# Softmax sums by matmuls, and HGRN2 keys and queries relative to chunk references, in a hybrid encoder layer

## The chip, the core and the metric

The kernel runs on one core of a Trainium2 chip. The metric is device time in microseconds (us) of one execution; less is better. Engines are named as the profile names them: PE (matrix engine; PEld is its weight load), DVE (vector), ACT (scalar, activation functions), POOL (GpSimd), SP (issues most of the DMAs).

## What is computed

One layer of an encoder for 512 tokens of width 1024. Two branches read the same normalised input: grouped-query attention with 8 heads of 64 and 2 key/value heads, and a gated linear recurrence (HGRN2) with 4 heads of 128, run once forward and once backward. Both are gated, added, projected and added to the input; a mixture of 32 experts in 4 groups follows. The change touches the softmax and the recurrence:

```
p = softmax(q k^T * scale);  o = p v                      # per head
f = lb + (1 - lb) * sigmoid(z);  k = (1 - lb) * sigmoid(-z)
b = cumsum(log f) within chunks of 32;  b_ref = b[16];  b_last = b[31]
a = (q * exp(b - b_ref)) (k * exp(b_ref - b))^T, masked;  o_intra = a v
o_inter = (q * exp(b)) state;  state = exp(b_last) * state + (k * exp(b_last - b))^T v
```

## The kernel before

Input projections come first, as products of float32 numbers split into a high and a low float32r part, three matmuls per product (`mm3`, L257 to L260; weights are split by ACT on L250 and DVE on L251). Then a loop over four HGRN heads h (L631) does for each h: the attention scores of heads 2h and 2h+1 (`att_scores`), the recurrence forward and backward (`hgrn_dir`), some other projections, the attention output of the pair (`att_out`), and the recurrence's output. Then come the branch projections with their gates, the output projection, the router, and the experts, whose 1 MB weight pieces are streamed through a ring of buffers as matmuls free them.

The program is written in this order, but a scheduler orders the instructions of PE, DVE, ACT and POOL ahead of time by its own estimate of durations; on the chip each engine then works strictly in that order. Only SP's queue stays as written.

In `att_scores` (L406) the keys lie on the partitions: four score tiles of 128 keys x 512 queries per head. DVE takes the maximum of the four (L423), POOL takes it over the partitions (`partition_all_reduce`, L424), DVE subtracts (L426) and ACT exponentiates (L427). For the denominator POOL adds the four tiles in pairs (L429, L430), DVE adds the two sums (L431), and one matmul with a matrix of ones adds over the partitions (L434). That matmul writes 64 of the 128 partitions, one half of the bank per head of the pair; ACT forms the reciprocal as exp(-ln) once for the pair (L437, L438). `att_out` multiplies the probabilities with v (L447, eight matmuls, the two heads alternating between the halves) and scales (L449).

In `hgrn_dir` (L505) the features lie on the partitions and the 512 tokens on the free axis: 4 blocks of 128 tokens with 4 chunks of 32 each. DVE clips the projection (L513), ACT forms log f in four passes (L514 to L517), POOL adds z and ln(1+exp(-z)) (L518), DVE sums within chunks by a scan (L520), which overwrites what L518 reads. Three exponent tiles follow (L530 to L534) and four wide exps (L532, L535 to L537): keys and queries relative to the chunk's reference (`z`, `e1`), keys to the chunk's end (`b`) and queries from its start (`e3`). One exp of the 16 chunk ends gives the chunks' decays T (L526), and POOL multiplies them up to the factors between the chunks of a block (L550 to L558). Scaled by them, keys and queries become `k2`, `q2`, `kt`, `qt` (L566 to L572). PE transposes `kt` (L586) and forms the blocks' states (L591). Back in the loop PE forms all decayed products between keys and queries in small matmuls (L661, L665), DVE masks them (L668 to L674), and PE forms the output (L685).

Of the kernel before, what the change touches and what calls it, by code (L numbers as in the profile page):

```python
# [11 lines left out]
ALU = mybir.AluOpType  # L12
# [92 lines left out]
def program_(tc, A, out, dbg=None):  # L105
# [41 lines left out]
    def ps(tag="b"):  # L147
        return tl(PS, [P, 512], tag, bufs=banks[tag])
# [254 lines left out]
    pq, den = [None], [None]  # L403
    probs = {}

    def att_scores(h):  # L406
# [22 lines left out]
        G.tensor_tensor(mx, sc[0], sc[1], op=ALU.add)  # L429
        G.tensor_tensor(mr, sc[2], sc[3], op=ALU.add)  # L430
        V.tensor_tensor(mx, mx, mr, op=ALU.add)  # L431
        if h % 2 == 0:
            den[0] = ps("po")
        PE.matmul(den[0][a], ones[:, 0:64], mx, start=True, stop=True)  # L434
        if h % 2 == 1:
            rc = at()
            SA.activation(rc, den[0], AF.Ln)  # L437
            SA.activation(rc, rc, AF.Exp, scale=-1.0)  # L438
            probs["r", h // 2] = rc
        probs[h] = sc  # L440

    def att_out(m):

        o = ps("po")
        for j in range(NT):
            for i in range(2):
                PE.matmul(o[HALF[i]], vt[:, j, m // 2], probs[2 * m + i][j], start=(j == 0), stop=(j == NT - 1))  # L447
        rc = probs["r", m]
# [44 lines left out]
    zero = tl(RH, [P, P], "zero")  # L493
    G.memset(zero, 0.0)

    FAC = [[tl(RH, [P, 2, 4, NT], "fac%d%d" % (d_, i)) for i in range(2)] for d_ in range(2)]
    for d_ in range(2):
        for i in range(2):
            G.memset(FAC[d_][i], 1.0)

    def c4(ap):

# [2 lines left out]
    def hgrn_dir(h, d_, q):  # L505
# [3 lines left out]
        z = tl(RH, [P, 512], "z", bufs=2)  # L509
        u = tl(RH, [P, 512], "k", bufs=2)  # L510
        b = tl(RH, [P, 512], "bb", bufs=2)
        p_ = proj_fm(3 * h + d_)
        V.tensor_scalar(z, p_, -ZMAX, None, op0=ALU.max)  # L513
        SA.activation(u, z, AF.Exp, scale=-1.0)  # L514
        SA.activation(b, u, AF.Ln, bias=1.0)
        SA.activation(u, b, AF.Exp, scale=-1.0)
        SA.activation(u, u, AF.Ln, bias=lb[:, d_, h:h + 1], scale=omb[:, d_, h:h + 1])  # L517
        G.tensor_tensor(z, z, b, op=ALU.add)  # L518
        bv, uv = (b, u) if fw else (b[:, ::-1], u[:, ::-1])
        V.tensor_tensor_scan(bv, scanm, uv, 0.0, op0=ALU.mult, op1=ALU.add)  # L520
# [7 lines left out]
        e1 = tl(RH, [P, 512], "e1", bufs=2)
        e3 = tl(RH, [P, 512], "e3", bufs=2)
        V.tensor_tensor(z, z, b, op=ALU.add)  # L530
        V.tensor_tensor(uc, bc_, b3(bc_[:, :, ir], 16, 32), op=ALU.subtract)
        SA.activation(e1, u, AF.Exp)  # L532
        V.tensor_tensor(uc, b3(bc_[:, :, it], 16, 32), zc, op=ALU.subtract)
        V.tensor_tensor(zc, b3(bc_[:, :, ir], 16, 32), zc, op=ALU.subtract)  # L534
        SA.activation(z, z, AF.Exp, bias=lo_)  # L535
        SA.activation(e3, b, AF.Exp)
        SA.activation(b, u, AF.Exp, bias=lo_)  # L537
        V.scalar_tensor_tensor(e1, q, SC_H, e1, op0=ALU.mult, op1=ALU.mult)
        V.scalar_tensor_tensor(e3, q, SC_H, e3, op0=ALU.mult, op1=ALU.mult)

        ch = [0, 1, 2, 3] if fw else [3, 2, 1, 0]
        t4 = T.rearrange("p (t c) -> p t c", c=4)
        t_ = [t4[:, :, c] for c in ch]
        fac = FAC[d_][h % 2]
        kf = [fac[:, 0, c] for c in ch]
        qf = [fac[:, 1, c] for c in ch]
        whole = tl(RH, [P, NT], "whole", bufs=2)

        def mul(o, x, y):
            G.tensor_tensor(o, x, y, op=ALU.mult)  # L550

        G.tensor_copy(kf[2], t_[3])
        G.tensor_copy(qf[1], t_[0])
        mul(kf[1], t_[3], t_[2])
        mul(qf[2], t_[0], t_[1])
        mul(kf[0], kf[1], t_[1])
        mul(qf[3], qf[2], t_[2])
        mul(whole, kf[0], t_[0])  # L558
# [8 lines left out]
        V.tensor_tensor(q2[:, :, ch[3] % 2], c4(e3)[:, :, ch[3]], b3(t_[2], NT, 32), op=ALU.mult)
# [3 lines left out]
        V.tensor_tensor(c4(kt), c4(b), b4(fac[:, 0].rearrange("p c t -> p t c")), op=ALU.mult)
        G.tensor_tensor(c4(qt), c4(e3), b4(fac[:, 1].rearrange("p c t -> p t c")), op=ALU.mult)  # L572
# [20 lines left out]
        V.tensor_copy(st[:, 0], pu[:, 0:P])  # L593
        for n_ in (1, 2):
            i = order[n_]
            V.scalar_tensor_tensor(st[:, n_], st[:, n_ - 1], whole[:, i:i + 1], pu[:, n_ * P:(n_ + 1) * P],
                                   op0=ALU.mult, op1=ALU.add)
        return e1, z, qt, st, blocks


    def gate(chunk):
# [625 lines left out]
```

## Time and profile before

| | |
|---|---|
| median of 3 runs | 982.7 us (977.29 to 982.86) |
| profiled execution | 979.89 us |
| its span | 978.0 us |
| mean granted PE clock | 0.967 |
| DMA moved | 246.52 MB |

The profile shows one execution. Its page gives the busy time of each engine, the span in 40 slices with a digit of busy share each, the granted PE clock, and groups of instructions by line. Views of the trace give the same for stretches of time, the waits of one engine for another, and single instructions in order of time. A float32 matmul is shown as two records. In a row of a group "x8 | 11.4, 1420 | 22.6 <-" means eight instructions, 11.4 us busy, 1420 ns each, 22.6 us of idle time of the engine ahead of them and what ended it.

### The profile page before, as it was taken

The page shows a single profiled execution, that of the slowest core. Times are in us where ns is not written, and L with a number is a line of the kernel's source. Part 1 is how long each engine was busy: PE and PEld are TensorE (multiplying, and loading weights), DVE is VectorE, ACT ScalarE, POOL GpSimd, SP SyncE. Part 2 cuts the span into 40 slices and gives each one's busy share as a digit, 9 for nine tenths or more (in the row PEclk, how much of TensorE's full clock was granted, in tenths as well). Part 3 has the DMA queues.
Part 4 walks back from the last instruction along what each step waited for, and adds up shares of the span by engine and source line. Part 5 has one row for each costly group of instructions (what it writes and reads, how often), then busy time and mean ns, then how long its engine had stood idle before and what let it go on. Part 6 is the DMA issues. An engine that isn't in the chain of part 4 may idle for free. (4 is left out here: it accounts for less than half of the span.)

```text
span 978.0 us, 12665 instructions
## 1 busy us (share of the span) xinstructions
PE 884.4 (90%) x5058; PEld 560.2 (57%) x5059; DVE 456.1 (47%) x804; ACT 276.8 (28%) x476; POOL 154.2 (16%) x174
## 2 busy tenths in 40 slices
PE   6899779798796999999779999999989989899896
PEld 5889667586573888889743444444334443343333
DVE  6999769696764445442532332322213222132214
ACT  6557646466563344442201000000000000000000
POOL 4543343342521001110100000000000000000000
PEclk9999979998897999999969999999999999999999
DMA  6212101111010223499459999999999999999994
GB/s 217 97 66 87 65 25 48 59 44 65 24 65 22 86 86 107 151 413 406 142 211 379 388 421 417 419 419 418 419 418 419 419 419 419 417 420 420 420 405 136
DMA packets 49647, 246.52 MB, mean 252 GB/s; under 512 B 7088, under 2 KB 12976, under 8 KB 25648
## 3 DMA queue, kind: packets, MB, share of 16 engines
q1 hardware_dynamic: 44160, 238.32, 60.9%
q0 software_dynamic: 2304, 4.20, 1.2%
q10 hardware_dynamic: 3120, 3.15, 0.9%
q8 instruction: 42, 0.69, 0.3%
q14 instruction: 21, 0.17, 0.0%
HBM read 245.64 MB, written 4.19 MB: 255 GB/s over the span
## 5 line engine op out<-in xcount | busy, mean ns | idle before, releaser
L1034 PE MATMUL b<-e,wr 128*64 128x512 f32 x728 | 204.6, 600 | 8.6 <-DMA e<-in_wu 8.2
L1034 PEld LDWEIGHTS b<-e,wr 128*64 128x64 f32 x728 | 61.3, 137 | 105.3 <-issue 86.0
L1041 ACT ACTIVATE gt<-b,sw 128x512 f32<-128x512 f32 x16 | 11.0, 687 | 328.7 <-PE b L1034 328.7
L1059 PE MATMUL b<-e,gt 128*64 128x512 f32 (+1 forms) x368 | 95.4, 576 | 8.0 <-DMA e<-in_wd 6.1
L260 PE MATMUL b<-x,wl 128*128 128x512 f32 x224 | 90.8, 406 | 3.3 <-DVE wl L251 3.3
L258 PE MATMUL b<-x,wh 128*128 128x512 f32 x224 | 90.5, 404 | 3.1 <-DVE hg L481 2.2
L1034 PE MATMUL b<-x,wr 128*64 128x512 f32 x264 | 90.5, 597 | 2.7 <-DMA x<-in_wu 2.7
L1062 DVE TENSOR_TENSOR t<-b,t 128x512 fp32r<-128x512 f32 (+1 forms) x33 | 22.2, 673 | 147.9 <-ACT t L1061 147.9
L259 PE MATMUL b<-x,wh 128*128 128x512 f32 x224 | 90.0, 402 | 0.0
L250 ACT ACTIVATE wh<-wr 128x1024 fp32r<-128x1024 f32 (+1 forms) x60 | 61.5, 1027 | 78.2 <-PE b L259 44.5
L251 DVE TENSOR_TENSOR wl<-wr,wh 128x1024 fp32r<-128x1024 f32 (+1 forms) x60 | 77.1, 1286 | 10.7 <-ACT wh L250 10.7
L1005 POOL DMA_INDIRECT xs<-xd,ix x16 | 16.2, 1014 | 335.8 <-DVE sw L1007 179.9
L1059 PEld LDWEIGHTS b<-e,gt 128*64 128x64 f32 x368 | 30.8, 137 | 60.0 <-issue 46.1
L1042 DVE SCALAR_TENSOR_TENSOR gt<-b,sw,gt 128x512 f32<-128x512 f32 x16 | 12.0, 751 | 105.7 <-PE b L1034 95.6
L258 PE MATMUL b<-wh,m 128*128 128x256 f32 x176 | 51.2, 294 | 10.4 <-ACT wh L250 6.2
L1059 PE MATMUL b<-x,gt 128*64 128x512 f32 x152 | 50.6, 594 | 3.6 <-DMA x<-in_wd 3.6
L259 PE MATMUL b<-wl,m 128*128 128x256 f32 x176 | 51.6, 294 | 2.1 <-DVE wl L251 1.9
L1061 ACT ACTIVATE t<-b 128x512 fp32r<-128x512 f32 (+1 forms) x33 | 19.3, 584 | 120.3 <-PE b L1059 120.3
L260 PE MATMUL b<-wh,m 128*128 128x256 f32 x176 | 51.0, 292 | 1.3 <-DVE m L185 1.3
L260 PEld LDWEIGHTS b<-x,wl 128*128 128x128 f32 x224 | 43.6, 195 | 14.7 <-DVE wl L251 4.6
L1078 PE MATMUL b<-t,wl 128*128 128x512 f32 (+1 forms) x132 | 51.4, 391 | 0.0
L1079 PE MATMUL b<-t,wl 128*128 128x512 f32 (+1 forms) x132 | 50.5, 384 | 0.4 <-DVE t L1062 0.4
(326 smaller groups left out, 1679.6 us busy)
## 6 DMA issues: line engine op xcount, KB each, us to landing
e<-in_wu SPq DMA_DIRECT2D x46, 1024.0 KB, 19.9
e<-in_wg SPq DMA_DIRECT2D x45, 1024.0 KB, 19.9
e<-in_wd SPq DMA_DIRECT2D x42, 1024.0 KB, 19.9
x<-in_wd SPq DMA_DIRECT2D x19, 1024.0 KB, 19.9
x<-in_wg SPq DMA_DIRECT2D x17, 1024.0 KB, 19.9
x<-in_wu SPq DMA_DIRECT2D x16, 1024.0 KB, 19.9
wr<-in_wfm SPq DMA_DIRECT2D x28, 512.0 KB, 3.5
wr<-in_wtok SPq DMA_DIRECT2D x12, 512.0 KB, 3.4
```

The costliest lines, as they stand in the source:

```text
L250: SA.activation(h_[:, ks], r[:, ks], AF.Copy)
L251: V.tensor_tensor(l_[:, ks], r[:, ks], f(h_)[:, ks], op=ALU.subtract)
L258: PE.matmul(o, ah, bh, start=first, stop=False)
L259: PE.matmul(o, ah, bl, start=False, stop=False)
L260: PE.matmul(o, al, bh, start=False, stop=last)
L1005: G.indirect_dma_start(xs[q % 2][:, b], None, xd[:, :], bass.IndirectOffsetOnAxis(ap=ix[:, b], axis=0), bounds_check=S - 1, oob_is_err=False)
L1034: PE.matmul(o[j * 64:(j + 1) * 64, :], hT[half][:, k, b * P + j * 64:b * P + (j + 1) * 64], ring[(n, e, half)](k), start=(half == 0 and k ...
L1059: PE.matmul(o[j * 64:(j + 1) * 64, 0:w], hidT[:, k * P + j * 64:k * P + (j + 1) * 64], ring[("wd", e, n)](k)[:, c:c + w], start=(k == 0), ...
L1061: SA.activation(y[:, 2 * n, c:c + w], o[:, 0:w], AF.Copy)
L1062: V.tensor_tensor(y[:, 2 * n + 1, c:c + w], o[:, 0:w], f(y)[:, 2 * n, c:c + w], op=ALU.subtract)
L1078: PE.matmul(p_[:, 0:w], l, y[:, 2 * n, c:c + w], start=(i == 0), stop=False)
L1079: PE.matmul(p_[:, 0:w], l, y[:, 2 * n + 1, c:c + w], start=False, stop=(i == len(ys) - 1))
```

## The change

*Softmax.* The additions L429 to L431 and the two single matmuls per pair are taken out. `att_out` now accumulates the denominators: for each of the four key tiles and each head of the pair, a matmul with ones, into the bank that the transposed queries use (`pq`, one buffer). Ln and Exp follow, then the output matmuls.

*Keys and queries.* The scan writes over `z` instead of the logarithms. Only two wide exps remain: of b - b_ref and of its negative. The keys come from POOL's product of exp(-z) and sigmoid(z), times (1 - lb). The decays between chunks are formed as logarithms: POOL copies the chunk ends, DVE scans them over the block and adds the references, POOL subtracts three sets of differences, and ACT takes one exp of 72 numbers per partition. Keys and queries of all chunks (`kt`, `qt`) and those of the products between chunks (`k2`, `q2`, now two and three chunks wide) are scaled by these.

```
     def att_out(m):
-        o = ps("po")
+        o, den = ps("po"), ps("pq")
+        for j in range(NT):
+            for i in range(2):
+                PE.matmul(den[HALF[i]], ones[:, 0:64], probs[2 * m + i][j], start=(j == 0), stop=(j == NT - 1))
+        rc = at()
+        SA.activation(rc, den, AF.Ln)
+        SA.activation(rc, rc, AF.Exp, scale=-1.0)
...
     def hgrn_dir(h, d_, q):
...
-        SA.activation(u, b, AF.Exp, scale=-1.0)
-        SA.activation(u, u, AF.Ln, bias=lb[:, d_, h:h + 1], scale=omb[:, d_, h:h + 1])
-        G.tensor_tensor(z, z, b, op=ALU.add)
-        bv, uv = (b, u) if fw else (b[:, ::-1], u[:, ::-1])
-        V.tensor_tensor_scan(bv, scanm, uv, 0.0, op0=ALU.mult, op1=ALU.add)
+        SA.activation(s_, b, AF.Exp, scale=-1.0)
+        SA.activation(b, s_, AF.Ln, bias=lb[:, d_, h:h + 1], scale=omb[:, d_, h:h + 1])
+        G.tensor_tensor(u, u, s_, op=ALU.mult)
+        zv, bv = (z, b) if fw else (z[:, ::-1], b[:, ::-1])
+        V.tensor_tensor_scan(zv, scanm, bv, 0.0, op0=ALU.mult, op1=ALU.add)
...
+        V.tensor_tensor(b.rearrange("p (c s) -> p c s", s=32), zc, b3(zc[:, :, ir], 16, 32), op=ALU.subtract)
+        SA.activation(e1, b, AF.Exp)
+        SA.activation(s_, b, AF.Exp, scale=-1.0)
...
+        G.tensor_copy(ends[:, :, 1:5], way(c4(z)[:, :, :, it]))
+        V.tensor_tensor_scan(L[:, 0:NT * 5], starts.rearrange("p t c -> p (t c)"), ends.rearrange("p t c -> p (t c)"),
+                             0.0, op0=ALU.mult, op1=ALU.add)
+        R = Y[:, :, 4:8]
+        V.tensor_tensor(R, way(c4(z)[:, :, :, ir]), X[:, :, 0:4], op=ALU.add)
+        G.tensor_tensor(Y[:, :, 0:4], X[:, :, 4:5].to_broadcast([P, NT, 4]), R, op=ALU.subtract)
+        G.tensor_tensor(Y[:, :, 8:11:2], R[:, :, 1:4:2], R[:, :, 0:3:2], op=ALU.subtract)
+        G.tensor_tensor(Y[:, :, 11:13], R[:, :, 2:3].to_broadcast([P, NT, 2]), R[:, :, 0:2], op=ALU.subtract)
+        SA.activation(E, L, AF.Exp)
...
+        V.scalar_tensor_tensor(e1, q, SC_H, e1, op0=ALU.mult, op1=ALU.mult)
+        V.scalar_tensor_tensor(u, u, omb[:, d_, h:h + 1], s_, op0=ALU.mult, op1=ALU.mult)
...
+        V.tensor_tensor(c4(kt), c4(u), b4(way(EY[:, :, 0:4])), op=ALU.mult)
+        G.tensor_tensor(c4(qt), c4(e1), b4(way(EY[:, :, 4:8])), op=ALU.mult)
+        V.tensor_tensor(k2, c4(u)[:, :, 0:2] if fw else c4(u)[:, :, 2:4], b4(way(EY[:, :, 11:13])), op=ALU.mult)
+        V.tensor_tensor(q2, c4(e1)[:, :, 1:4] if fw else c4(e1)[:, :, 0:3], b4(way(EY[:, :, 8:11])), op=ALU.mult)
```

The matmuls of the recurrence keep their number and shapes. In the changed file L518 becomes L524 (POOL's product), L520 L526, L434 L435 and L447 L441; the copy of the ends is L540, the small scan L541, the three subtractions L545 to L547, the masks L663 to L669, the transposes L581, and L685 L680.

The scheduler's order moves with it. On POOL, around the all-reduces of attention heads 2 and 3 (`at`), before; ISA rows are instructions of POOL's own:

```order
L424 ISA
L424 ISA at_1394<-at_1393 128x512
L429 ISA
L429 TENSOR_TENSOR at_1393<-m_1389,m_1390 128x512
L430 TENSOR_TENSOR at_1394<-m_1391,m_1392 128x512
L424 ISA
L424 ISA at_1560<-at_1559 128x512
L429 ISA
L429 TENSOR_TENSOR at_1559<-m_1555,m_1556 128x512
L430 TENSOR_TENSOR at_1560<-m_1557,m_1558 128x512
```

and in the changed kernel:

```order
L424 ISA
L424 ISA at_1389<-at_1388 128x512
L424 ISA at_1542<-at_1541 128x512
L524 ISA
L524 TENSOR_TENSOR k_1967<-k_1967,sg_1969 128x512
L540 COPY end_135_837<-z_1966 128x4x4
L545 TENSOR_TENSOR log_131_833<-log_131_833 128x4x4
```

With the additions gone the two all-reduces follow each other, and what comes behind them is the product and the copy for the next forward direction. The same holds for heads 6 and 7; heads 0, 1, 4 and 5 keep other POOL work between.

On DVE, between the first pair's output and the second forward direction (`as` and `zb` are the masked products, `m` the score tiles), before:

```order
L513 TENSOR_SCALAR z_1466<-b_1475 128x512
L670 COPY_PREDICATED as_1346<-c_maskf_282,zero_831 128x512
L426 TENSOR_TENSOR m_1015<-m_1015,at_1020 128x512
L426 TENSOR_TENSOR m_1016<-m_1016,at_1020 128x512
L426 TENSOR_TENSOR m_1017<-m_1017,at_1020 128x512
L426 TENSOR_TENSOR m_1018<-m_1018,at_1020 128x512
L520 SCALAR_TENSOR_TENSOR bb_1468<-c_scanm_286,k_1467 128x512
L668 COPY_PREDICATED zb_829<-c_maskb_284,hg_1281 128x128
L530 TENSOR_TENSOR z_1466<-z_1466,bb_1468 128x512
L531 TENSOR_TENSOR k_1467<-bb_1468 128x512
L674 TENSOR_TENSOR as_1346<-as_1346,zb_829 32x4x32 x4
```

and in the changed kernel:

```order
L663 COPY_PREDICATED zb_829<-c_maskb_284,hg_1276 128x128
L665 COPY_PREDICATED as_1341<-c_maskf_282,zero_831 128x512
L669 TENSOR_TENSOR as_1341<-as_1341,zb_829 32x4x32 x4
L426 TENSOR_TENSOR m_1013<-m_1013,at_1018 128x512
L426 TENSOR_TENSOR m_1014<-m_1014,at_1018 128x512
L426 TENSOR_TENSOR m_1015<-m_1015,at_1018 128x512
L426 TENSOR_TENSOR m_1016<-m_1016,at_1018 128x512
L519 TENSOR_SCALAR z_1456<-b_1467 128x512
L251 TENSOR_TENSOR wl_1654<-wr_1649,wh_1653 128x1024
L526 SCALAR_TENSOR_TENSOR z_1456<-c_scanm_286,bb_1458 128x512
L529 TENSOR_TENSOR bb_1458<-z_1456 128x512
L541 SCALAR_TENSOR_TENSOR log_132_834<-starts_841,end_136_838 128x20
```

The masks moved ahead of the subtractions and the scan; the small scan that needs POOL's copy stands behind the large one.

On PE, the last pair's sums and outputs (`po` and `pq` are the banks, `m` the probability tiles, `sc` a branch projection, `hg` the recurrence's output), before:

```order
L665 MATMUL hg_2905<-e_455_2705,z_2662 32x32 x16
L434 MATMUL po_2492<-at_2625,ones_82 64x512
L447 MATMUL po_2892<-m_2455,vt_161 64x512
L447 MATMUL po_2892<-m_2621,vt_161 64x512
L447 MATMUL po_2892<-m_2456,vt_161 64x512
L447 MATMUL po_2892<-m_2622,vt_161 64x512
```

and in the changed kernel, behind one matmul of each kind 50 rows earlier:

```order
L260 MATMUL sc_2973<-t_827,wl_2955 128x512
L435 MATMUL pq_2828<-m_2571,ones_82 64x512
L435 MATMUL pq_2828<-m_2419,ones_82 64x512
L441 MATMUL po_2827<-m_2571,vt_161 64x512
L441 MATMUL po_2827<-m_2419,vt_161 64x512
L435 MATMUL pq_2828<-m_2572,ones_82 64x512
L435 MATMUL pq_2828<-m_2420,ones_82 64x512
L441 MATMUL po_2827<-m_2572,vt_161 64x512
```

The sums now read the probabilities (`m`) instead of POOL's and DVE's sum (`at`), stand behind 18 branch matmuls, and are mixed with the outputs.

More of the change, by code (lines that the diff above doesn't have):

```diff
@@ L402, in program_ @@
     aTh, aTl = [tl(U, [P, 4, 512], "t", F32R, bufs=2) for _ in range(2)]
-    pq, den = [None], [None]
+    pq = [None]
     probs = {}
@@ L427, in att_scores @@
             SA.activation(sc[j], sc[j], AF.Exp, scale=0.125)
[L429 to L439, printed above, removed]
         probs[h] = sc
     def att_out(m):
-        o = ps("po")
+        o, den = ps("po"), ps("pq")
[5 more added lines that the diff above has]
+        SA.activation(rc, rc, AF.Exp, scale=-1.0)
         for j in range(NT):
@@ L494, in program_, with logs @@
     G.memset(zero, 0.0)
-    FAC = [[tl(RH, [P, 2, 4, NT], "fac%d%d" % (d_, i)) for i in range(2)] for d_ in range(2)]
+    LOGS = [[tl(RH, [P, NT * 18], "log%d%d" % (d_, i)) for i in range(2)] for d_ in range(2)]
+    ENDS = [[tl(RH, [P, NT, 5], "end%d%d" % (d_, i)) for i in range(2)] for d_ in range(2)]
+    starts = tl(RH, [P, NT, 5], "starts")
+    G.memset(starts, 1.0)
+    G.memset(starts[:, :, 0], 0.0)
     for d_ in range(2):
         for i in range(2):
-            G.memset(FAC[d_][i], 1.0)
+            G.memset(LOGS[d_][i], 0.0)
+            G.memset(ENDS[d_][i], 0.0)
+    def logs(t):
+        return (t[:, 0:NT * 5].rearrange("p (t c) -> p t c", c=5), t[:, NT * 5:].rearrange("p (t c) -> p t c", c=13))
     def c4(ap):
@@ L528, in hgrn_dir @@
[L528 to L558, printed above, removed]
+        V.tensor_tensor(b.rearrange("p (c s) -> p c s", s=32), zc, b3(zc[:, :, ir], 16, 32), op=ALU.subtract)
+        SA.activation(e1, b, AF.Exp)
+        SA.activation(s_, b, AF.Exp, scale=-1.0)
+        L, ends = LOGS[d_][h % 2], ENDS[d_][h % 2]
+        X, Y = logs(L)
@@ new lines, in hgrn_dir, with way @@
+        E = tl(RH, [P, NT * 18], "fac", bufs=2)
+        def way(ap):
+            return ap if fw else ap[:, :, ::-1]
+        G.tensor_copy(ends[:, :, 1:5], way(c4(z)[:, :, :, it]))
[4 more added lines that the diff above has]
+        G.tensor_tensor(Y[:, :, 0:4], X[:, :, 4:5].to_broadcast([P, NT, 4]), R, op=ALU.subtract)
@@ L572, in hgrn_dir @@
-        G.tensor_tensor(c4(qt), c4(e3), b4(fac[:, 1].rearrange("p c t -> p t c")), op=ALU.mult)
+        k2 = tl(RH, [P, NT, 2, 32], "k2", bufs=2)
+        q2 = tl(RH, [P, NT, 3, 32], "q2", bufs=2)
+        V.tensor_tensor(c4(kt), c4(u), b4(way(EY[:, :, 0:4])), op=ALU.mult)
+        G.tensor_tensor(c4(qt), c4(e1), b4(way(EY[:, :, 4:8])), op=ALU.mult)
+        V.tensor_tensor(k2, c4(u)[:, :, 0:2] if fw else c4(u)[:, :, 2:4], b4(way(EY[:, :, 11:13])), op=ALU.mult)
+        V.tensor_tensor(q2, c4(e1)[:, :, 1:4] if fw else c4(e1)[:, :, 0:3], b4(way(EY[:, :, 8:11])), op=ALU.mult)
@@ L574, in hgrn_dir @@
+        ch = [0, 1, 2, 3] if fw else [3, 2, 1, 0]
+        i1, i23, i3 = (0, slice(1, 3), 2) if fw else (2, slice(0, 2), 0)
+        j0, j1 = (0, 1) if fw else (1, 0)
         blocks = []
@@ L595, in hgrn_dir @@
             i = order[n_]
-            V.scalar_tensor_tensor(st[:, n_], st[:, n_ - 1], whole[:, i:i + 1], pu[:, n_ * P:(n_ + 1) * P],
+            V.scalar_tensor_tensor(st[:, n_], st[:, n_ - 1], EX[:, i, 4:5], pu[:, n_ * P:(n_ + 1) * P],
                                    op0=ALU.mult, op1=ALU.add)
-        return e1, z, qt, st, blocks
+        return e1, u, qt, st, blocks
     def gate(chunk):
```

26 lines of the change are left out of this document (9 added, 17 removed).

## Prediction

> **What bounds the kernel now.** I read the page first, for the span and the stages, then busy time by stretch, then PE's waits, then POOL and DVE where those waits point.
>
> ```profile
> span 978.0 us, 12665 instructions
> PE 884.4 (90%) x5058; PEld 560.2 (57%) x5059; DVE 456.1 (47%) x804; ACT 276.8 (28%) x476; POOL 154.2 (16%) x174
> PE   6899779798796999999779999999989989899896
> PEclk9999979998897999999969999999999999999999
> DMA  6212101111010223499459999999999999999994
> ```
>
> One digit is 24.5 us. The changed code lies in digits 4 to 13 (about 80 to 317 us), where PE is neither idle nor full, its clock dips three times, and DMA is at one or two tenths. Behind digit 20 DMA is at nine. By stretch (busy us of PE, PEld, DVE, ACT, POOL, then clock, DMA share, GB/s):
>
> ```profile
> 120.00:160.00 40.00, 31.38 (x264) 24.81 (x265) 31.02 (x47) 20.04 (x36) 18.87 (x24) 0.87 0.12 40
> 280.00:320.00 40.00, 30.33 (x249) 19.76 (x248) 21.27 (x48) 15.61 (x28) 6.85 (x5) 0.87 0.12 42
> 320.00:360.00 40.00, 40.00 (x184) 33.15 (x183) 18.23 (x24) 16.30 (x23) 0.00 (x0) 1.00 0.28 99
> 440.00:480.00 40.00, 38.98 (x332) 38.69 (x331) 13.26 (x29) 9.74 (x27) 1.41 (x1) 1.00 0.68 271
> 520.00:978.00 458.00, 428.22 (x2038) 185.18 (x2037) 126.04 (x240) 29.59 (x48) 13.88 (x14) 1.00 0.98 400
> ```
>
> The expert stage is bound by its weight stream (0.98 of the DMA engines). Ahead of it the DMA share is 0.68, so the weights that can be fetched early don't hold it up, and from 320 us PE is full at clock 1.00. So whatever PE saves before 320 us should reach the end one for one: the stream starts when PE's work frees its buffers, and its length doesn't change. What holds PE up before that:
>
> ```profile
> PE po L434 <- DVE at L431: 17.9, 5, 5.5
> PE hg L685 <- DVE as L674: 7.1, 1, 7.1
> PE hg L665 <- ACT as L667: 2.5, 1, 2.5
> PE b L260 <- DVE wl L251: 2.2, 2, 1.8
> PE b L258 <- DVE hg L481: 2.2, 1, 2.2
> PE hg L586 <- DVE kt L571: 1.0, 1, 1.0
> ```
>
> These are PE's waits from 80 to 330 us (total us, times, longest). Half of the wait is L434, the matmul that adds up the softmax. POOL shows why it is late (start, us, idle before):
>
> ```profile
> 126.68 1.80 POOL L424 PARTITION_ALL_REDUCE at<-at  x1 [5.90 <-DVE as L670]
> 135.36 1.25 POOL L518 TENSOR_TENSOR z<-z,bb 128x512 f32<-128x512 f32 x1 [6.87 <-issue]
> ...
> 292.25 1.80 POOL L424 PARTITION_ALL_REDUCE at<-at  x1 [5.98 <-issue]
> 301.25 1.25 POOL L429 TENSOR_TENSOR at<-m,m 128x512 f32<-128x512 f32 x1 [7.21 <-issue]
> 302.48 1.25 POOL L430 TENSOR_TENSOR at<-m,m 128x512 f32<-128x512 f32 x1
> ```
>
> Each all-reduce has about 5.9 us of idle POOL before it and about 7 behind it; the order of instructions has an extra row (ISA) at both places, and POOL's queue shows changes of its configuration at the all-reduce, two rows for each of the eight:
>
> ```profile
> L424 POOLq MODIFY_POOL_CONFIG  x16: 1/6/14, 99.7 to 286.5; - x16
> ```
>
> The additions L429 and L430 sit behind the second gap, so the last head's sum comes 9.7 us after its maximum (294.05 to 303.73).
>
> **The change part by part.** (1) *The denominators.* L429 to L431 go; the sums of the four probability tiles are accumulated by ones matmuls instead, which need only the exponentials. The wait of 17.9 us goes with it. It costs more than itself, for the clock falls behind PE's long waits:
>
> ```profile
> 120.00:128.00 8.00, 6.44 (x84) 4.73 (x85) 5.26 (x9) 3.06 (x5) 2.10 (x2) 0.79 0.19 68
> 144.00:152.00 8.00, 8.00 (x51) 6.64 (x50) 8.00 (x10) 5.42 (x11) 4.57 (x5) 0.86 0.19 66
> 176.00:184.00 8.00, 7.50 (x113) 5.72 (x112) 6.98 (x13) 5.11 (x9) 1.80 (x1) 0.79 0.19 68
> 224.00:232.00 8.00, 6.31 (x16) 4.99 (x17) 6.71 (x9) 4.63 (x8) 5.01 (x4) 0.57 0.19 69
> 248.00:256.00 8.00, 5.56 (x33) 3.24 (x34) 6.20 (x9) 3.56 (x6) 3.94 (x10) 0.57 0.00 0
> 304.00:312.00 8.00, 6.74 (x18) 1.71 (x18) 1.80 (x6) 1.23 (x2) 0.00 (x0) 0.62 0.01 2
> ```
>
> Behind the den waits, (1 - clock) x 8 us is 1.7 at 120, 1.7 at 176, 3.4 at 248 and 3.0 at 304: 9.8 us. [...]
>
> The new matmuls have the shape of L447, and the old ones ran alone (start, us):
>
> ```profile
> 146.98 1.07 PE L434 MATMUL po<-at,ones 128*64 128x512 f32 x2
> 151.52 3.65 PE L447 MATMUL po<-m,vt 128*64 128x512 f32 x16
> ```
>
> Eight single sums took 8 x 1.07 = 8.6 us. Eight matmuls whose two output halves alternate took 3.65, so the two halves overlap. Four pairs of heads give 4 x 3.65 = 14.6; in the new order the first matmul of the sum and the first of the output stand alone ahead of the rest, which I put at 1 us per pair: 18.6, so +10.0 us of PE. Bounds: +6.0 if nothing is lost (14.6 - 8.6), +25.6 if no halves overlap (32 x 1.07 - 8.6). I stay near the low end, since the rows alternate halves in the order printed above.
>
> Ln and Exp of the denominators come later, beside the output's matmuls, by the row of L437 (80 to 330 us: busy us, mean ns, idle before):
>
> ```profile
> L437 ACT ACTIVATE at<-po 128x512 f32<-128x512 f32 x4 | 2.4, 594 | 9.1 <-PE po L434 8.3 <-POOL qt L572 0.8
> ```
>
> The output's matmuls (3.65 us) cover these two passes; without that cover they cost 1.2 us at four places.
>
> (2) *The scan no longer waits for POOL.* L518 must have read the logarithms before the scan L520 overwrites them, so POOL's second gap ran through DVE's queue into the masks (L674) and PE (L685):
>
> ```profile
> DVE at L431 <- POOL at L430: 26.1, 7, 4.9
> DVE bb L520 <- POOL z L518: 5.6, 1, 5.6
> ```
>
> In the new code the scan writes over z, POOL's product (L524) touches neither, and the masks stand ahead of the subtractions that wait for the all-reduce. I count L685's 7.1, L665's 2.5 and the 1.1 us of slow clock in the stretch at 144: 10.7 us. DVE also stops standing 26.1 us at L431.
>
> (3) *Keys and queries.* Per direction DVE loses L530, L533, L534 (rows of 80 to 330 us: busy us, mean ns):
>
> ```profile
> L530 DVE TENSOR_TENSOR z<-z,bb 128x512 f32<-128x512 f32 x8 | 6.4, 794 | 0.1
> L533 DVE TENSOR_TENSOR k<-bb,z 128x512 f32<-128x512 f32 x8 | 8.4, 1056 | 0.1
> L534 DVE TENSOR_TENSOR z<-bb,z 128x512 f32<-128x512 f32 x8 | 5.4, 680 | 0.0
> L567 DVE TENSOR_TENSOR q<-e,T 128x128 f32<-128x128 f32 x8 | 3.6, 452 | 0.0
> L553 POOL COPY fac<-T 128x4 f32<-128x4 f32 x8 | 4.4, 550 | 0.0
> L550 POOL TENSOR_TENSOR fac<-T 128x4 f32<-128x4 f32 x16 | 5.3, 354 | 0.0
> L518 POOL TENSOR_TENSOR z<-z,bb 128x512 f32<-128x512 f32 x8 | 11.4, 1420 | 22.6 <-DVE wl L251 12.0 <-issue 6.9 <-ACT bb L515 3.7
> ```
>
> That is 20.2 us for all eight, of which about 4 comes back by wider k2 and q2 and two tiny operations. ACT loses two passes of 512 per direction. None of it is on PE's path by itself: worth nothing while PE is the last to be ready, though it stands behind the waits on wl, hg and kt (2.2, 2.2, 1.0) and the slow clock at 224 (3.4), 8.8 us in all. Against it stands a longer chain to the factors: POOL copies the ends (0.55), DVE scans and adds (0.45 each at most, by L567), POOL subtracts three times (3 x 0.354), ACT takes one exp, some 3 us, and k2, which needed only T before, now waits for it. After an all-reduce the copy also stands behind POOL's 7 us and the product (1.42). New waits lie between 0 and, for three forward directions behind a gap (3 x 11.4) and five others (5 x 3), 49 us, less up to 8.8 that DVE's relief may bring. I take 4 us lost: in PE's order some 50 to 60 rows lie between a forward projection's end and the transposes that need its keys, at the 0.22 us of the stretch from 320 us (184 in 40.00) some 12 us, about as long as gap and chain.
>
> (4) *POOL's configuration.* Two pairs of all-reduces now follow each other directly (heads 2 and 3, 6 and 7): six changes there and back instead of eight. This makes the last pair's probabilities earlier, and is why I let L434's whole wait go.
>
> **The sum.** 17.9 + 9.8 + 10.7 = 38.4 saved; 10.0 + 4.0 lost; 24.4 net. The profiled execution took 979.9 us, 1.9 more than its span, so 979.9 - 24.4 = 955.5, say 955. The median of the three runs is 982.7; the profiled time lies inside their spread. With the bounds of (1), and up to 20 of the 49 us of (3), the case runs from 979.9 - 38.4 + 6.0 - 8.8 = 939 to 979.9 - 38.4 + 10 + 20 = 972.
>
> **The rivals.** *PE stays full and warm:* the wl, hg and kt waits go too and every slow stretch with them. Quoted waits 32.9, clock 14.3 (1.1 and 3.4 more than the four above), less 10 for the matmuls: 979.9 - 37.2 = 943. For it: DVE has over 40 us more room. Against: the order is still fixed ahead of time, with POOL's gaps in it.
>
> *The wait moves:* the second head's exponentials wait for the all-reduce, and PE stands at the first new matmul that needs them. If that gives back 17.9 + 9.8 it is 955.5 + 27.7 = 983, no change. For it: for the first and third pair the all-reduce still has a change of configuration ahead of it. Against: between that head's scores and those matmuls stand some 70 rows, half of them large, so 8 to 15 us, where maximum, all-reduce, subtraction and exp need 4 (1.80 and three passes of 0.6 to 0.7), and 10 with the gap. That the weight stream starts no earlier, so that the saving is lost later (980), belongs here too; the 0.68 above speaks against it.
>
> *Slower:* the factors' chain becomes what PE waits for. Behind each of the three gaps PE stands 11.4 us at the transposes of kt and then runs 3.4 us' worth slow, and 3 us in the five other directions: 3 x 14.8 + 15 = 59 instead of the 4 counted, 955.5 + 55 = 1011. It decides once these waits pass 28 us, about half of that. For it: DVE now stands at the small scan for POOL's copy with the rest of its queue behind it. Against: before, the whole long chain (scan, four wide DVE operations, exponentials) began only after the gap; now most of it runs during it.
>
> **How the numbers follow.** Forecast 0.62, full and warm 0.18, wait moved or lost later 0.11, slower 0.09. Faster by over 1% (about what a measurement of this kernel can tell from no change) means under 973: 0.62 + 0.18 = 0.80; within 1% 0.11; slower 0.09. The range of 8 in 10 takes in the warm case and the upper end of the forecast with some of the moved wait: 937 to 976.
>
> **What would show it.** Right: no PE wait over 2 us on the denominators and none on the masks; no wait of the scan on POOL; fewer than 16 configuration rows at the all-reduce; the first expert matmul (L1034) about 24 us earlier and the stretch behind it unchanged at 0.98 DMA. Step (1) is wrong if PE waits for ACT's exponentials there or the 64 new records don't pair; step (3) if PE waits for kt, k2 or q2, or DVE for POOL's copy by more than a few us each. The forecast as a whole fails if the expert stretch grows by what the first part saves.

## The result and the profile after

The changed kernel takes 954.65 us (median of 4 runs, 953.46 to 955.93). On the same chip the kernel before takes 982.53; the ratio, taken over all timed runs and not from the two medians, is 0.9726 with a 95% interval of 0.9696 to 0.9756. The profiled execution took 953.46 us.

The page of the changed kernel, span, busy times and clock (slices of 23.8 us):

```profile
span 951.7 us, 12689 instructions
PE 885.9 (93%) x5106; PEld 558.7 (59%) x5107; DVE 438.6 (46%) x788; ACT 267.3 (28%) x460; POOL 125.7 (13%) x132
PE   6899989998999999999599999999989989799896
PEclk9999989999999999999699999999999999999999
```

PE's busy time is the same as before within 1.5 us, in a span that is 26.3 us shorter, so the gain shows as idle time (93.6 us before, 65.8 now). Busy time includes matmuls at a slow clock: less of that and the added matmuls about cancel, as the account below shows. The 7s and the 6 in digits 5 to 13 of PE's row (counted from 1) are gone, and of the clock's dips a small one at digit 6 is left, and the one ahead of the experts (digit 20, before 21), which is behind the changed code. PE's waits from 80 to 312 us in the changed kernel (total us, times, longest):

```profile
PE pq L435 <- ACT m L427: 6.7, 2, 3.9
PE hg L660 <- DVE st L591: 1.7, 1, 1.7
PE sc L420 <- DVE at L423: 0.7, 1, 0.7
PE sc L258 <- DVE m L623: 0.3, 1, 0.3
```

They add up to 9.4 us; those of before add up to 35.6 in the same stretch. No wait for the masks is left. The denominators still stop PE, at two places and for another reason: PE is ready for the new sums before the second head's exponentials are. PE's timeline shows both (start, us, idle before):

```profile
126.41 6.18 PE L435 MATMUL pq<-m,ones 128*64 128x512 f32 x13 [2.84 <-ACT m L427]
...
227.76 4.92 PE L435 MATMUL pq<-m,ones 128*64 128x512 f32 x13 [3.89 <-ACT m L427]
```

Those are the first and the third pair of heads. POOL's timeline has the cause at the first:

```profile
104.74 1.80 POOL L424 PARTITION_ALL_REDUCE at<-at  x1 [5.67 <-DVE wl L251]
114.08 3.27 POOL L481 TENSOR_TENSOR hg<-hg,c_hnorm 128x256 f32<-128x256 f32 x4 [7.54 <-issue]
123.17 1.80 POOL L424 PARTITION_ALL_REDUCE at<-at  x1 [5.82 <-issue]
```

Between the two all-reduces POOL multiplies four tiles by the HGRN norm (L481). That takes 3.27 us itself, but costs a gap of 7.54 ahead and 5.82 behind. DVE has the second head's maximum ready at 115.74 us, 7.4 us before POOL starts on it. At the third pair the gaps are 6.95 and 5.90, with one product for `qt` (L561, 1.05 us) and L481 (3.83 us) between them, and the maximum waits 8.4 us for POOL. Where nothing stands between them, as for heads 2 and 3, no change of configuration does:

```profile
157.42 1.80 POOL L424 PARTITION_ALL_REDUCE at<-at  x1 [5.92 <-issue]
167.23 1.78 POOL L424 PARTITION_ALL_REDUCE at<-at  x1 [8.01 <-DVE at L423]
```

The second one's idle time is a wait for DVE's maximum. The configuration rows are down from 16 to 12:

```profile
L424 POOLq MODIFY_POOL_CONFIG  x12: 4/8/11, 99.0 to 257.1; - x12
```

The clock falls behind the two waits only (windows of 8 us, columns as before):

```profile
120.00:128.00 8.00, 5.16 (x26) 3.52 (x26) 3.00 (x5) 2.27 (x4) 1.80 (x1) 0.85 0.00 0
128.00:136.00 8.00, 8.00 (x26) 2.44 (x22) 5.78 (x8) 5.10 (x9) 3.44 (x5) 0.72 0.19 66
224.00:232.00 8.00, 4.24 (x12) 1.31 (x13) 5.50 (x12) 3.75 (x6) 1.80 (x1) 0.79 0.00 0
```

(1 - clock) x 8 us over all such windows from 80 to 312 us comes to 5.1, against 20.5 before. The expert stage starts earlier and runs as it did. Its first matmul in the kernel before and in the changed one, and then the same 424 us of it in both:

```profile
L1034 PE MATMUL b<-e,wr x728: 592/592/1112, 502.7 to 952.3; 128*64 128x512 f32 x182
```

```profile
L1029 PE MATMUL b<-e,wr x728: 592/592/1116, 477.2 to 925.9; 128*64 128x512 f32 x182
```

```profile
546.00:970.00 424.00, 401.13 (x1893) 173.07 (x1893) 114.45 (x210) 27.71 (x45) 11.90 (x12) 1.00 0.99 406
```

```profile
520.00:944.00 424.00, 401.72 (x1907) 175.24 (x1907) 115.69 (x213) 27.70 (x45) 11.87 (x12) 1.00 0.99 407
```

The first matmul comes 25.5 us earlier, the end 26.3.

### The profile page after: what moved, and what is told of

Its sections match the earlier page's. It is cut to its first block, busy times and chain, and to the rows that moved or that the text cites. A ratio compares the mean times of both kernels' runs of the same rounds, so it can differ in the third digit from the quotient of the medians.

```text
span 951.7 us, 12689 instructions
## 1 busy us (share of the span) xinstructions
PE 885.9 (93%) x5106; PEld 558.7 (59%) x5107; DVE 438.6 (46%) x788; ACT 267.3 (28%) x460; POOL 125.7 (13%) x132
## 5 line engine op out<-in xcount | busy, mean ns | idle before, releaser
L260 PE MATMUL b<-x,wl 128*128 128x512 f32 x224 | 88.2, 394 | 1.0 <-DVE wl L251 1.0
L258 PE MATMUL b<-x,wh 128*128 128x512 f32 x224 | 88.1, 393 | 0.8 <-ACT hv L330 0.8
L259 PE MATMUL b<-x,wh 128*128 128x512 f32 x224 | 88.0, 393 | 0.0
L258 PE MATMUL b<-wh,m 128*128 128x256 f32 x176 | 51.6, 297 | 10.6 <-ACT wh L250 6.5
L1029 PEld LDWEIGHTS b<-x,wr 128*64 128x64 f32 x264 | 26.3, 136 | 38.5 <-issue 32.9
## 6 DMA issues: line engine op xcount, KB each, us to landing
e<-in_wu SPq DMA_DIRECT2D x46, 1024.0 KB, 19.9
e<-in_wg SPq DMA_DIRECT2D x45, 1024.0 KB, 19.9
e<-in_wd SPq DMA_DIRECT2D x42, 1024.0 KB, 19.9
x<-in_wd SPq DMA_DIRECT2D x19, 1024.0 KB, 19.9
x<-in_wg SPq DMA_DIRECT2D x17, 1024.0 KB, 19.9
```

The costliest lines, as they stand in the source:

```text
L258: PE.matmul(o, ah, bh, start=first, stop=False)
L259: PE.matmul(o, ah, bl, start=False, stop=False)
L260: PE.matmul(o, al, bh, start=False, stop=last)
L1029: PE.matmul(o[j * 64:(j + 1) * 64, :], hT[half][:, k, b * P + j * 64:b * P + (j + 1) * 64], ring[(n, e, half)](k), start=(half == 0 and k ...
```

## One account for all runs

To compare kernels whose waits lie at different lines, each profiled execution is put into one account: its span, less all of PE's waits from 80 to 312 us, less the clock lost there, (1 - clock) x 8 us summed over 29 windows. What is left is the time that the same execution would take with PE never waiting and never slow in that stretch. It is an estimate, since a wait and a slow clock can stand for each other, but it is the same for all. Medians and ratios are those of the timed runs, the other columns of the profiled execution. Each ratio is to runs of the kernel before that were timed beside that kernel (medians 980.5 to 982.5 us), so between rows the ratios compare better than the medians.

| kernel | median | ratio to before (95%) | span | PE waits | clock lost | left |
|---|---|---|---|---|---|---|
| before | 982.7 | 1 | 978.0 | 35.6 | 20.5 | 921.9 |
| e2 keys and queries alone | 982.71 | 1.0008 (0.9991 to 1.0026) | 978.3 | 39.4 | 18.7 | 920.2 |
| e5 before, scan in its own tile | 982.10 | 1.0012 (1.0000 to 1.0023) | 982.4 | 37.5 | 19.9 | 925.0 |
| e8 keys and queries, sums on DVE | 960.04 | 0.9809 (0.9775 to 0.9843) | 956.8 | 20.9 | 13.6 | 922.3 |
| e3 before, sums on DVE | 956.84 | 0.9759 (0.9733 to 0.9786) | 954.7 | 18.2 | 8.5 | 928.0 |
| e10 e3 and norm on DVE | 948.53 | 0.9685 (0.9668 to 0.9701) | 945.2 | 11.8 | 6.8 | 926.6 |
| e1 softmax alone | 966.96 | 0.9863 (0.9833 to 0.9893) | 964.5 | 15.5 | 8.4 | 940.6 |
| after | 954.65 | 0.9726 (0.9696 to 0.9756) | 951.7 | 9.4 | 5.1 | 937.2 |
| e9 softmax, scan in its own tile | 950.98 | 0.9702 (0.9687 to 0.9716) | 949.2 | 4.3 | 1.7 | 943.2 |
| e11 after, more DVE work | 956.87 | 0.9763 (0.9746 to 0.9780) | 954.3 | 10.6 | 3.4 | 940.3 |
| e7 after, logarithms on DVE | 950.33 | 0.9716 (0.9678 to 0.9755) | 948.1 | 6.9 | 3.4 | 937.8 |
| e6 after, norm on DVE | 947.07 | 0.9667 (0.9631 to 0.9703) | 945.7 | 4.0 | 1.7 | 940.0 |
| c1 after, norm and logarithms on DVE | 944.79 | 0.9638 (0.9619 to 0.9657) | 943.1 | 2.1 | 0.0 | 941.0 |
| e4 after, denominators summed twice | 976.84 | 0.9969 (0.9945 to 0.9992) | 972.6 | 15.0 | 6.8 | 950.8 |

The last column falls into three groups. Without the added matmuls it is 920 to 928 (mean 924.0), with them 937 to 943 (mean 940.0), with them doubled 951. So by this estimate the added matmuls cost about 16 us, and what the change takes away is 41.6 us of waits and slow clock (56.1 to 14.5).

## The experiments

**e1: the softmax part alone.** The kernel before with the change's `att_scores` and `att_out`; `hgrn_dir` as it was.

```diff
-        G.tensor_tensor(mx, sc[0], sc[1], op=ALU.add)
-        G.tensor_tensor(mr, sc[2], sc[3], op=ALU.add)
-        V.tensor_tensor(mx, mx, mr, op=ALU.add)
...
+        for j in range(NT):
+            for i in range(2):
+                PE.matmul(den[HALF[i]], ones[:, 0:64], probs[2 * m + i][j], start=(j == 0), stop=(j == NT - 1))
```

> The kernel before with only the softmax part of the change. Theory (most of the gain is the denominators' way past POOL): 17.9 us of PE wait and 9.8 us of slow clock go, 10 us of matmuls come, so 960 to 973; the wait on the masks (7 us) may stay. Rival (the gain comes from the lighter work for keys and queries on DVE and POOL): 976 to 990, since PE then only has more to do.

966.96 us. PE does not wait for the denominators at all, but now for the keys' transposes, and DVE's scan for POOL (first PE's wait, then DVE's):

```profile
PE hg L579 <- DVE kt L564: 6.9, 3, 4.0
```

```profile
DVE bb L513 <- POOL z L511: 15.8, 3, 5.5
```

About half of the gain is the softmax part's own. The scan stood 5.6 us behind POOL's sum in the kernel before; now that PE is no longer held up elsewhere it stands 15.8.

**e2: the keys' and queries' part alone.** The change's `hgrn_dir` in the kernel before, softmax as it was.

> The kernel before with only the keys and queries part of the change; the denominators still go through POOL's and DVE's additions and one matmul per head. Theory: the scan's and the masks' wait goes (10.7 us), a few us come back by the longer chain, and PE still waits 10 to 18 us for the denominators, so 970 to 980. Rival (lighter DVE and POOL are the gain): 955 to 965.

982.71 us: no change, which neither theory had. PE's waits:

```profile
PE po L434 <- DVE at L431: 18.1, 5, 7.7
PE b L258 <- ACT hv L473: 8.8, 1, 8.8
...
PE hg L588 <- DVE kt L567: 3.0, 1, 3.0
```

The masks stop PE for only 1.1 us instead of 7.1, as the theory said, but the wait for the denominators is as long as before, and a new wait of 8.8 us stands behind the longer chain to the factors. ACT's timeline shows it:

```profile
166.38 0.26 ACT L555 ACTIVATE fac<-log 128x72 f32<-128x72 f32 x1 [9.29 <-POOL log L554]
```

ACT stands 9.29 us at the factors' exp for POOL's last subtraction, which comes only after POOL's gap of 6.84 us behind an all-reduce. The copy of `hv` that PE needs stands behind that exp in ACT's order. So what the masks gave was taken by the change's own chain.

**e5: the scan in a tile of its own.** The smallest edit that takes POOL out of the scan's way, with the softmax and the keys and queries as before (the scan writes a new buffer instead of the one that POOL reads; the queries' temporary `zq` now shares the two buffers of `z`, as in the changed kernel).

```diff
-        b = tl(RH, [P, 512], "bb", bufs=2)
+        b = tl(RH, [P, 512], "bb", bufs=3)
...
         G.tensor_tensor(z, z, b, op=ALU.add)
+        b = tl(RH, [P, 512], "bb", bufs=3)
         bv, uv = (b, u) if fw else (b[:, ::-1], u[:, ::-1])
...
-        zq = tl(RH, [P, 512], "zq", bufs=1)
+        zq = tl(RH, [P, 512], "z", bufs=2)
```

> The kernel before with the scan writing a tile of its own, so that it need not wait for POOL's addition to have read the logarithms; nothing else of the change. Theory: the masks' wait of 7 us and its slow clock go, 970 to 977. Rival (the next DVE operation, which needs POOL's sum, takes the wait over): 980 to 985, with PE's wait on the masks still there or moved.

982.10 us, in the rival's range. The scan waits for POOL nowhere and the wait for the masks is gone, but PE's waits as a whole are no shorter (37.5 us, 35.6 before): those at the denominators grew by 8.5.

```profile
PE po L434 <- DVE at L431: 26.4, 6, 6.5
```

By itself, taking away the scan's wait is worth nothing.

**e3: the sums on DVE.** No matmul added, keys and queries as before; only the two additions change engine.

```diff
-        G.tensor_tensor(mx, sc[0], sc[1], op=ALU.add)
-        G.tensor_tensor(mr, sc[2], sc[3], op=ALU.add)
+        V.tensor_tensor(mx, sc[0], sc[1], op=ALU.add)
+        V.tensor_tensor(mr, sc[2], sc[3], op=ALU.add)
```

> The kernel before with the two POOL additions of the denominators done by DVE instead (16 additions of 128x512, about 11 us more on DVE); no matmul is added. Theory (POOL's change of configuration is what makes the sums late): the wait goes as with the ones matmuls, and their 10 us of PE are not paid, so 952 to 966. Rival (the sums are late because they stand in a vector engine's queue at all, and only PE can take them off): 974 to 986.

956.84 us, the change's whole gain within the intervals, by two changed lines. PE's waits:

```profile
PE b L258 <- ACT wh L250: 6.9, 1, 6.9
...
PE po L434 <- DVE at L431: 1.0, 1, 1.0
```

DVE does each addition in 0.68 us, POOL did it in 1.27 behind a gap of 7. So it was the additions' place on POOL that held the denominators up, not the additions. Their place costs in two ways that this run does not separate: the gap ahead of them, and the changes of configuration that they cause (12 rows here, 16 before).

**e4: the denominators twice.** The changed kernel with every ones matmul done twice and the logarithm's input halved.

```diff
-        for j in range(NT):
+        for j in range(2 * NT):
             for i in range(2):
-                PE.matmul(den[HALF[i]], ones[:, 0:64], probs[2 * m + i][j], start=(j == 0), stop=(j == NT - 1))
+                PE.matmul(den[HALF[i]], ones[:, 0:64], probs[2 * m + i][j % NT], start=(j == 0), stop=(j == 2 * NT - 1))
...
-        SA.activation(rc, den, AF.Ln)
+        SA.activation(rc, den, AF.Ln, scale=0.5)
```

> The changed kernel with every ones matmul of the denominators done twice into the same sum (64 instead of 32; Ln halves its argument). Theory (PE is what bounds this stage after the change, so matmuls cost their time): 4 x 3.65 = 14.6 us more than the changed kernel, 966 to 973. Rival (the matmuls run while PE would wait anyway): 955 to 961.

976.84 us, 22 us above the changed kernel and more than even the theory had. Of the 20.9 us between the spans, 5.6 are PE's waits, 1.7 clock and 13.6 the rest, which I put down to the matmuls. The sums' groups from 80 to 330 us, of this kernel and of c1, where PE hardly waits:

```profile
L435 PE MATMUL pq<-m,ones 128*64 128x512 f32 x128 | 35.4, 605 | 10.9 <-ACT m L427 10.7
L441 PE MATMUL po<-m,vt 128*64 128x512 f32 x64 | 23.0, 608 | 0.0
```

```profile
L441 PE MATMUL po<-m,vt 128*64 128x512 f32 x64 | 20.6, 594 | 0.0
L435 PE MATMUL pq<-m,ones 128*64 128x512 f32 x64 | 20.1, 603 | 0.3 <-ACT m L427 0.3
```

**e6: the norm's products on DVE.** The changed kernel without L481 between the all-reduces of the first and of the third pair. At the third the product for `qt` (L561) stays between them on POOL.

```diff
-                G.tensor_tensor(ov, ov, hnorm.unsqueeze(1).to_broadcast([P, 2, P]), op=ALU.mult)
+                V.tensor_tensor(ov, ov, hnorm.unsqueeze(1).to_broadcast([P, 2, P]), op=ALU.mult)
```

> The changed kernel with the products of gate and norm weight (eight of 128x256) on DVE instead of POOL, so that the all-reduces of heads 0 and 1 follow each other without a change of configuration; heads 4 and 5 keep one. Theory (what PE still waits for is the exponentials behind such a change, 6.7 us and 5 us of slow clock at two places, one of which is mended): 947 to 952. Rival (the wait moves to other work of DVE): 953 to 958.

947.07 us. All its runs lie below all of the changed kernel's, though the intervals of the two ratios just overlap. Ten configuration rows, and the wait for the exponentials is 0.6 us instead of 6.7:

```profile
L424 POOLq MODIFY_POOL_CONFIG  x10: 1/5/14, 99.6 to 250.9; - x10
```

```profile
PE pq L435 <- ACT m L427: 0.6, 1, 0.6
```

So the two waits that the change left came from L481's place on POOL. Only at the first pair did the change of configuration go with it; at the third the two gaps stay (7.22 and 5.78 us), and POOL is spared L481's 3.83 us alone, about as much as PE had waited there (3.89).

**e7: the logarithms of the ends on DVE.** The changed kernel with L540 and L545 to L547 on DVE.

```diff
-        G.tensor_copy(ends[:, :, 1:5], way(c4(z)[:, :, :, it]))
+        V.tensor_copy(ends[:, :, 1:5], way(c4(z)[:, :, :, it]))
...
-        G.tensor_tensor(Y[:, :, 0:4], X[:, :, 4:5].to_broadcast([P, NT, 4]), R, op=ALU.subtract)
+        V.tensor_tensor(Y[:, :, 0:4], X[:, :, 4:5].to_broadcast([P, NT, 4]), R, op=ALU.subtract)
```

The other two subtractions are moved alike.

> The changed kernel with the copy of the chunk ends and the three small subtractions on DVE instead of POOL, so that the chain to the factors goes from DVE to ACT without POOL and its change of configuration. Theory (nothing waits for that chain in the changed kernel): 952 to 958. Rival (the longer chain costs what I had put down, 4 us or more): 944 to 951.

950.33 us, in the rival's range, but its interval overlaps that of the changed kernel. Waits on the exponentials fell only from 6.7 to 6.4 us. Inconclusive, at most some 4 us.

**e8: keys and queries with the sums on DVE.** e2 and e3 together: the whole change except that DVE does the sums, without added matmuls.

> The keys and queries part of the change, with the denominators as before but POOL's two additions done by DVE; no ones matmuls beyond the one per head. Theory (the gain is that POOL is no longer between exponentials and denominators, and the matmuls cost 10 us of PE): 943 to 950, faster than the whole change. Rival (DVE, with 11 us more, becomes what PE waits for, so that the matmuls are worth their time): 955 to 965.

960.04 us, as the rival had it. The spared matmuls do not show, because waits took their place. PE's first three:

```profile
PE hg L588 <- DVE kt L567: 7.1, 1, 7.1
PE po L434 <- DVE at L431: 5.6, 3, 2.4
PE b L258 <- ACT wh L250: 4.4, 1, 4.4
```

and what leads to the first, DVE's wait for the factors and POOL's first subtraction for them:

```profile
DVE kt L567 <- ACT fac L555: 4.8, 1, 4.8
```

```profile
210.28 0.21 POOL L552 TENSOR_TENSOR log<-log 128x16 f32<-128x16 f32 x1 [6.81 <-issue]
```

That is the chain to the factors by the change's new operations (subtractions on POOL, here behind its gap after an all-reduce, and the exp), the rival "slower" of the prediction on a small scale.

**e9: the softmax part with the scan in a tile of its own.** e1 with e5's edit. Keys and queries as before.

> The kernel before with the softmax part alone (967.0, where DVE's scan stood 15.8 us for POOL's sum), and the scan writing a tile of its own, so that it need not wait for POOL's sum of logarithms. Keys and queries as before. Theory: the 12 us that the keys' and queries' part adds on top of the softmax part come from this wait: 953 to 961. Rival: they come from DVE's lighter work (five wide passes fewer in a direction, three wider or new): 963 to 970, no better than the softmax part alone.

950.98 us, below the theory's range and, within the intervals, all that the changed kernel has, from the softmax part and three lines. DVE's only waits for POOL, then PE's two longest (4.3 us in all):

```profile
DVE z L524 <- POOL z L511: 3.3, 3, 1.1
...
DVE m L426 <- POOL at L424: 0.9, 1, 0.9
```

```profile
PE b L258 <- DVE hg L474: 2.2, 1, 2.2
PE sc L258 <- ACT t L443: 1.4, 1, 1.4
```

The scan's wait for POOL and PE's for kt are both gone. The same edit that gave nothing in e5 gives 16 us here (966.96 to 950.98). One reservation: each edit lets the scheduler order the instructions anew, and this kernel has 12 configuration rows where e1 has 14.

**e10: the sums and the norm on DVE.** e3 with e6's edit.

> The kernel before with the sums over keys' blocks on DVE instead of POOL (956.8 alone), and the product with the HGRN norm on DVE too. No matmul added, keys and queries as before. Theory: POOL's queue around the all-reduces sets the stage, and the norm's products stand in it here as in the changed kernel, where moving them gave 7.6 us: 946 to 953. Rival: without the added matmuls nothing waits there (PE stood only 1.0 us at the sums in that kernel): 954 to 960.

948.53 us, with 8 configuration rows. Its remaining waits are scattered over nine lines, 11.8 us in all; the two longest:

```profile
PE b L260 <- DVE wl L251: 2.9, 1, 2.9
PE po L434 <- DVE at L431: 2.5, 2, 1.7
```

It is as fast as e6 within the intervals, without one added matmul and with the old keys and queries.

**e11: more work for DVE.** The changed kernel with a reduction nobody reads, three times in each direction. It computes the same outputs.

```diff
+        xs = tl(RH, [P, 16], "xs", bufs=1)
+        for _ in range(3):
+            V.tensor_reduce(xs, b.rearrange("p (c s) -> p c s", s=32), axis=AX.X, op=ALU.max)
         SA.activation(e1, b, AF.Exp)
```

> The changed kernel with three more passes of DVE over 512 elements in each of the eight directions, whose output nobody reads: 24 x 0.68 us (a reduction of this size in the changed kernel's groups) = 16 us more DVE work in the first part, which more than gives back what the keys' and queries' part took from DVE. Theory: that part helped by taking POOL out of the scan's way, and DVE has room: 953 to 959. Rival: it helped by making DVE's share lighter: 963 to 972.

956.87 us. 16 us of DVE work cost 2.2 us by the medians (3.6 by the ratios), and the intervals overlap. So DVE's lighter share is not what the keys' and queries' part mended, with one reservation: the order moved here too (10 configuration rows instead of 12), which may hide some of the cost.

**c1: norm and logarithms on DVE.** e6 and e7 together.

> The changed kernel with both edits that take work from POOL: the product with the HGRN norm and the small copy and subtractions on the logarithms of the ends go to DVE. Each alone gave 947.1 and 950.3. Theory: what is left of PE's waits in this stage hangs on POOL's place, at two places that have nothing to do with each other, so most of both gains adds up: 941 to 948. Rival: both took away the same wait (the exponentials behind the first all-reduces), or DVE now gets full: 948 to 956.

944.79 us, the fastest kernel here, though not told apart from e6 (the intervals overlap). PE's two longest waits (2.1 us in all) and the whole stretch:

```profile
PE sc L258 <- ACT t L443: 1.3, 1, 1.3
PE pq L435 <- ACT m L427: 0.3, 1, 0.3
```

```profile
80.00:312.00 232.00, 229.77 (x1659) 176.46 (x1658) 174.36 (x329) 137.30 (x231) 41.47 (x24) 1.00 0.18 60
```

PE is full and its clock whole. Nothing more is to be had in this stretch from waits; only less PE work would help.

## Why the prediction was right, and where its steps were not

The time was within half a microsecond, and that closeness is luck, because errors of opposite sign met. Of the 26.3 us between the spans the account gives 41.6 saved and 15.3 lost; the prediction had 38.4 and 14.0. Term by term, the waits gave 26.2 (27.5 counted), the slow clock 15.4 (10.9 counted), the matmuls cost about 16 (10.0 counted), and of the 4.0 for the longer chain nothing shows.

*Where the gain would go* was right: whatever PE saves ahead of the experts reaches the end. The first expert matmul is 25.5 us earlier (about 24 were expected), and the expert stretch did not change.

*Step (1), the denominators.* The mechanism is shown by e3 and e1: POOL's place, and the clock behind the wait. But by the prediction's own sign this step fails in part, for PE does wait for ACT's exponentials there, and three numbers were off. The wait did not go whole: the step let 17.9 us go by reason of step (4), but (4) mends only the second and fourth pair, and at the first and third 6.7 us came back, with 5.1 us of slow clock behind it. That is the mechanism of the rival "the wait moves", at 11.8 us instead of its 27.7. Against that rival the prediction had set 8 to 15 us of PE's work between the second head's scores and the new matmuls, and a need of 10 us with the gap. The work was 11.9 and 11.2 us, as set; the need was 14.7 and 15.1, because the maximum also waited 7.4 and 8.4 us for POOL, which had L481 to do first. The sign "no PE wait over 2 us on the denominators" was wrong, with 2.84 and 3.89. The clock gave 15.4 back (20.5 to 5.1), not the 9.8 here and 1.1 in step (2), since I priced single windows of 8 us: the slow phases at 144 and at 304 us began in the windows ahead of these, with 2.3 and 2.1 us more. Two phases that I had left out of the sum, at 102 and 224 us, went too (1.7 and 3.4), about as much as came new. And the matmuls cost about 16 us, not 10.0: in c1, at full clock, sums and outputs take 20.1 + 20.6 = 40.7 us of groups, against 10.5 + 16.0 = 26.5 before (rows below), and e4 adds 13.6 by the second set. I had added 14.6 + 4 for sums mixed with outputs; the sums came near that, 20.1, but the outputs between them grew by 4.6.

```profile
L447 PE MATMUL po<-m,vt 128*64 128x512 f32 x64 | 16.0, 646 | 0.7 <-ACT at L437 0.7
L434 PE MATMUL po<-at,ones 128*64 128x512 f32 x16 | 10.5, 744 | 18.0 <-DVE at L431 17.9
```

*Step (2), the scan.* The mechanism is there: in the changed kernel the scan waits for POOL nowhere and the masks stop PE nowhere. The addition was wrong. I added 10.7 us as if this wait and that of the denominators were two bills. They are two stops on one road: PE arrives at L434 earlier by what it saves at the masks and stands there instead. e5 shows it, 0 us, and e9 shows the other side, 16 us once L434 is out of the way. e2 gains nothing either, but there the chain of step (3) takes what the masks give. Here a wait was worth its length only once the next stop behind it was no longer set by the same late engine.

*Step (3), keys and queries.* I counted 4 us lost. e9 against the changed kernel is what this part costs beyond the scan's freedom: 3.7 us between the medians, but the intervals overlap. Nothing shows that the keys' and queries' arithmetic gained anything by itself, and e11 speaks against its lighter DVE work as a cause of more than a few us. That work was over-counted too: e2 has 9.0 us less DVE time than the kernel before, not 16. The long chain to the factors is real in e2 (8.8 us behind ACT, 3.0 at the transposes) and in e8 (7.1 at the transposes); in the changed kernel PE does not wait for kt, and DVE not for POOL's copy.

*Step (4), the configuration.* Twelve rows instead of sixteen, as read from the order. It did not make the last head early everywhere, as said under (1).

*The rivals.* Full and warm (943) is what c1 is, at 944.79 us, but two more edits were needed for it. No change and slower did not come.

Open: whether e10's sums on DVE together with e9's scan tile would run below c1. By the account 924 to 928 are left there, 13 to 17 below c1, but e8 shows how waits fill such room; it was not tried. How much of each edit's effect is the scheduler's new order rather than the edit itself was not separated either.

## What to carry to other kernels

On an engine that works in order, ask first what else stands in its queue between an operation and the one that needs its result: two cheap additions on POOL (1.25 us each for the last head, behind a gap of 7.21 at a change of configuration) held the matrix engine up, waits and slow clock together, by more than the some sixteen microseconds of matmuls that replaced them, and moving them to DVE did as well (956.84 us against 954.65). Do not add up the waits of one engine as if each were a bill of its own; take away the one that stands last on the chain, and measure the others again. An edit that gives nothing alone (e5) may be worth most once the wait behind it is gone (e9), so a null result is a statement about the kernel around it.

## What the runs showed of the hardware

*A change of configuration on POOL* went in the changed kernel with 5.67 to 5.92 us of idle POOL ahead of the all-reduces shown above, and 7.54 behind one until the next ordinary operation (L481). The gap behind is the larger one here.

*The slow clock came and went in steps of one length here.* Stretches of 0.4 us at the edges of both slow phases of the changed kernel:

```profile
125.20:125.60 0.40, 0.00 (x0) 0.00 (x0) 0.40 (x1) 0.00 (x0) 0.00 (x0) 0.98 0.00 0
125.60:126.00 0.40, 0.00 (x0) 0.00 (x0) 0.40 (x2) 0.27 (x1) 0.00 (x0) 0.50 0.00 0
...
132.40:132.80 0.40, 0.40 (x4) 0.14 (x1) 0.40 (x1) 0.00 (x0) 0.40 (x1) 0.98 0.00 0
227.60:228.00 0.40, 0.23 (x2) 0.20 (x4) 0.40 (x2) 0.40 (x2) 0.00 (x0) 0.98 0.00 0
228.00:228.40 0.40, 0.40 (x2) 0.00 (x0) 0.40 (x2) 0.40 (x2) 0.00 (x0) 0.50 0.00 0
...
231.20:231.60 0.40, 0.40 (x4) 0.10 (x2) 0.40 (x1) 0.00 (x0) 0.00 (x0) 0.75 0.00 0
```

The first phase runs from 125.6 to 132.4 us, the second from 228.0 to 231.4: 6.8 and 3.4 us, with a granted clock of 0.50 inside. The first began 2.0 us after PE stopped (126.41 - 2.84 = 123.57), in a wait of 2.84 us in all; the second began 0.2 us after PE had started again (227.76), behind a wait of 3.89. The two starts lie 102.4 us apart. In the kernel before, in steps of 0.1 us, the slow phases between 100 and 320 us begin at 101.9, 122.4, 139.4, 177.0, 224.8, 248.6 and 299.8 us and last 3.4, 3.4, 6.8, 3.4, 6.8, 6.9 and 10.3 us. The 197.9 us from the first of these starts to the last are about 58 times the shortest phase, which gives steps of 3.412 us (an estimate from these numbers). In them the other six starts lie 6, 11, 22, 36, 43 and 58 steps behind the first within 0.1 us, and the two starts in the changed kernel lie 30 steps apart. Why the starts lie so, the runs do not show. The phases at 122.4 and 177.0 came behind stops of 2.81 and 2.68 us at L434, so the two terms of 1.7 us in step (1) were rightly counted. A stop of 1.69 us (113.51 to 115.20 in the changed kernel) left the clock whole. So a stop of under three microseconds (2.84) was followed here by 6.8 us at half speed, which cost another 3.4, and one of 3.89 by 3.4 us, which cost 1.7.
